# Four small edits in a transformer layer: where head sums are stored from, when ACT's tables are loaded, how the last projection fetches its heads, and how the last store leaves

## The chip, the cores and the metric

The kernel runs on one core of a Trainium2 chip. The metric is the device time of one execution in microseconds. Matrix products run on TensorE (PE), elementwise work on VectorE (DVE), ScalarE (ACT) and GpSimd (POOL), and almost all DMA requests are issued by SyncE (SP), whose queue works in order: a request that waits for its data holds up those behind it. Each engine takes its instructions in the order in which the program wrote them.

## The reference

One encoder layer over a sequence of 2048 rows with 1024 features, all in float32.

```python
mod = c_act @ w_ada[l] + b_ada[l]
sh1, sc1, gt1, sh2, sc2, gt2 = [m[:, None, :] for m in jnp.split(mod, 6, axis=-1)]
h = rmsnorm(x, g_norm1[l]) * (1.0 + sc1) + sh1
proj = h @ w_in[l]
q_sb, k_sb, v_sb, q_ca, k_ca, v_ca = jnp.split(proj, split_pts, axis=-1)
o_sb = stick_breaking_attention(hs(q_sb, ...), hs(k_sb, ...), hs(v_sb, ...))   # 8 heads, strictly causal
o_ca = chunked_relpos_attention(q_ca, k_ca, hs(v_ca, ...), rel_bias[l])        # 8 heads, 9 chunks of 64
mixed = jnp.concatenate([o_sb.reshape(B, S, D_SB), o_ca.reshape(B, S, D_CA)], axis=-1)
x = x + gt1 * (mixed @ w_o[l])
h = rmsnorm(x, g_norm2[l]) * (1.0 + sc2) + sh2
x = x + gt2 * (jnp.square(jax.nn.relu(h @ w1[l])) @ w2[l])
```

## The kernel before, in words

Everything is held transposed, features on partitions, and the sequence is cut into four blocks of 512 (`TB`), called groups `g`. A float32 operand is cut into a high and a low part (`split`: ACT writes the high part, another engine subtracts), and a product is three matmuls (`mm3`). There are three stages.

**Input projections**, up to about 415 us. **Attention**, up to 1285 us: a list of units, each a head `h` and a group `g` (stick-breaking `SB` or chunked `CA`), is worked through in steps, four to a unit. In a step PE makes scores and transposes of weights, ACT a sigmoid (`SB`) or an exponential (`CA`), DVE a scan or a reduction, and POOL a difference or a scaling. Dense matmuls (the rest of the projections, and the output projections `outproj` of groups 3, 2 and 1) are spread into the steps by `fill`; their results leave through tiles `st` of the pool `fp`. Work that has to come later stands in lists: `soon` is done in the next step, `later` counts steps, with its `tick` at a step's end. When both heads of a pair are done, `finish` copies them out of PSUM on ACT, `total` adds two tiles `o` and `otmp` on POOL, and `keep` splits the sum into the tile `os` and stores it to DRAM as `scr_m[g, pair]`. In the kernel before, `os` has one buffer. A step is `turned` where the units change from `SB` to `CA` or back; that is three times, and ACT then needs another table.

**After attention** ("last projection" and MLP). The remaining rows of `outproj` of group 1 are worked off by `row()`, each 24 matmuls `po<-fx,ow`. Between them the requests for the next work are issued: `steps[0].fetch` loads the eight head tiles `opm` of group 0 from `scr_m`, 512 KB each, for the last projection (`Mixed`, matmuls `pso<-opm`), and `some(0, 0)` loads four tiles `ty` of 256 KB with rows of the residual for the first block of the MLP's input. `some(0, 1)` then multiplies and splits them into `h` (`right_blocks`: `scale`, `mixed`, `rest`; four blocks `k`, of which the first works on `ty` and the others on `cy`). While PE runs the eight rows of `Mixed`, DVE and ACT make the four blocks and store residual rows in between; the first products of the MLP (`First`) need all four blocks and a weight split `opr`. The MLP is computed with seven products of a 2x2 block scheme (`PRODUCTS`), `First` and `Second`, twice (`mb` 1, 0). In the last step of `Second` four results `tx` are added on DVE, one after the other, and stored to `out`.

The orders here are written out by hand: after attention every engine's instruction is pinned behind the one written before it, SP's requests too. DMA requests use eight completion semaphores in turn.

Of the kernel before, what the change touches and what calls it, by code (L numbers as in the profile page):

```python
# [10 lines left out]
F32R = mybir.dt.float32r  # L11
BF16 = mybir.dt.bfloat16
AF = mybir.ActivationFunctionType
# [5 lines left out]
P = 128  # L19
# [5 lines left out]
KT = D // P  # L25
TB = 512
# [53 lines left out]
def encoder_kernel(ctx, tc, xT, c, g1, g2, w_in, w_rest, gqk, bias, w_o, w1, w2, w_ada, b_ada, out):  # L80
    nc = tc.nc
    act, dve, pool, sp = nc.scalar, nc.vector, nc.gpsimd, nc.sync
# [35 lines left out]
    zero = cpool.tile([P, 1], F32, name="zero")  # L118
# [9 lines left out]
    cols = cpool.tile([P, 184], F32, name="cols")  # L128
# [7 lines left out]
    later = Later()  # L136

    def split(hi, lo, src, lo_eng=None):
        act.copy(hi, src)
        (lo_eng or dve).tensor_tensor(lo, src, hi.bitcast(F32), op=ALU.subtract)  # L140
# [63 lines left out]
    def mm3(ps, st_hi, st_lo, mv_hi, mv_lo, first, last, more=False):  # L204

        pe.matmul(ps, st_hi, mv_hi, start=first, stop=False, skip_group_check=more)
        pe.matmul(ps, st_hi, mv_lo, start=False, stop=False, skip_group_check=more)
        pe.matmul(ps, st_lo, mv_hi, start=False, stop=last, skip_group_check=more)
# [36 lines left out]
    if True:  # L245
# [257 lines left out]
        act, dve, pool = (Ordered(tc, e) for e in (act, dve, pool))  # L503
# [124 lines left out]
        sp = osp  # L628
# [77 lines left out]
    ph = ctx.enter_context(ExitStack())  # L706
    if True:
# [8 lines left out]
            out=held[:, :P], in_=held[:, :P], pattern=[[1, P]], base=0, channel_multiplier=-1,  # L716
# [4 lines left out]
        sp = nc.sync  # L721
# [33 lines left out]
        def total(u, o, tmp):  # L755

            pool.tensor_tensor(o, o, tmp, op=ALU.add)
            soon.append(lambda: soon.append(lambda: keep(u, o)))

        def keep(u, o):  # L760

            os = op.tile([P, 2, TB], F32R, tag="os", name=f"os{u.nm}", bufs=1)
            split(os[:, 0, :], os[:, 1, :], o, pool)
            q = act if u is units[-1] else sp
            q.dma_start(scr_m[u.g, u.ca * 4 + u.h // 2], os.bitcast(F32))
            pairs[u.g] += 1
            if pairs[u.g] == KT and u.g > 0:
                filler.append(Filler(outproj, u.g))
# [48 lines left out]
        class SB(Unit):  # L817
# [13 lines left out]
            def load(self):  # L831
                if self.first:
                    pend["q"] = load_q(0, self.h, self.g)
                    pend["last"] = [None] * 4
                self.q = pend["q"]
                self.carry = pend["last"]
                if pend.get("k0") != (self.h, self.c):
                    pend["k"] = kp0.tile([P, TB], F32R, tag="k0", name=f"k0{self.nm}")
                    load_k(0, self.h, self.c, 1, pend["k"])
                    pend["k0"] = self.h, self.c  # L840
                self.k = pend["k"]
# [338 lines left out]
        late, soon, first, second = [], [], [], []  # L1180
# [26 lines left out]
        def force(f):  # L1207

            got = next(f.gen, None)
            if callable(got):  # L1210
                got()
            return None if got is None else callable(got)
# [18 lines left out]
        def value(u, j):  # L1231
            u.values(j)
# [14 lines left out]
        op = ph.enter_context(tc.tile_pool(name="op", bufs=2))  # L1247
        pado = ph.enter_context(tc.tile_pool(name="pado", bufs=1))
        pado.tile([P, 80], F32, tag="pad", name="pado")
        fp = ph.enter_context(tc.tile_pool(name="fp", bufs=3))  # L1250
        wtp = ph.enter_context(tc.tile_pool(name="wtp", bufs=4))
        ldq = sp
        steps = [(u, st) for u in units for st in range(STEPS)]
        for i in range(len(steps) + LAG):
            if i % STEPS == 0:
                if i // STEPS + AHEAD < len(units):
                    load(units[i // STEPS + AHEAD])
            vi = i - VST
            if vi >= 0 and vi % STEPS == 0 and vi // STEPS < len(units):
                units[vi // STEPS].load_values()  # L1260
            front, fs = steps[i] if i < len(steps) else (None, 0)
            back, bs = steps[i - LAG] if i >= LAG else (None, 0)
            done = list(soon)
            soon.clear()
            js = []
            if back is not None:
                nb = len(back.banks)
                js = range(nb * bs // STEPS, nb * (bs + 1) // STEPS)
            for j in js:
                back.transposes(j)  # L1270
            turned = front is not None and i and front.ca != steps[i - 1][0].ca
            if front is not None and not turned:
                front.soft1(fs)
            while first:
                first.pop(0)()
            while second:
                second.pop(0)()
            for j in js:
                back.parts(j)
                late.append((back, j))  # L1280
            if turned:
                front.soft1(fs)
            if front is not None:
                front.soft2(fs)
            for job in done:
                if turned:
                    later.add(3, job)
                else:
                    job()
            while len(late) > AVLAG:  # L1290
                value(*late.pop(0))
            if i + 1 < len(steps):
                u, st = steps[i + 1]
                u.scores(st)
            fill(front.weight if front else 0.6, 6 if turned else 0)
            later.tick()
# [7 lines left out]
    sp = osp  # L1304
# [8 lines left out]
    HK = KT // 2  # L1313
# [5 lines left out]
    if True:  # L1319
# [21 lines left out]
        def column_sum(eng, out, a, b, op):  # L1341
            eng.tensor_tensor(out, a, b, op=op)
            return out
# [4 lines left out]
        def kept(nm):  # L1348
            return accp.tile([P, TB], F32, tag="c", name=f"c{nm}")

        def bank(nm):
            return pp.tile([P, TB], F32, tag="ps", name=f"ps{nm}")

        steps, jobs = [], {}
# [92 lines left out]
        class Step:  # L1447
# [5 lines left out]
            def run(self):  # L1453
                pass
# [120 lines left out]
        class Second(Step):  # L1575
# [27 lines left out]
            def run(self):  # L1603
                mb, i, j = self.mb, self.i, self.j
                if j == 0:
                    Second.banks[i] = [bank(f"{self.nm}_{n}") for n in range(HK)]
                if i not in (1, 6, 5):
                    if j == NP // 2 - 1:
                        self.load_base()
                    if NP // 2 + 2 < j <= NP // 2 + 2 + HK:  # L1610
                        self.base(j - NP // 2 - 3)
                for n in range(HK):
                    ns = slice(n * P, (n + 1) * P)
                    mm3(
                        Second.banks[i][n], self.w[:, 0, ns], self.w[:, 1, ns], self.h[:, 0, :], self.h[:, 1, :],
                        j == 0, j == NP - 1,
                    )
                if j == NP - 1:
                    for n in range(HK):
                        self.out(n, Second.banks[i][n])  # L1620

            def load_base(self):
                i, d = self.i, Second.whole
# [8 lines left out]
                x, u = d["x", n], d[{7: "v", 2: "s", 3: "v", 4: "u"}[i], n]  # L1632
                dve.scalar_tensor_tensor(x, u, mod[:, 5 * KT + nn : 5 * KT + nn + 1], x, op0=ALU.mult, op1=ALU.add)

            def out(self, n, ps):
                i, d = self.i, Second.whole
                tb = 2 * self.mb + (i in (2, 4))
                if i == 1:
                    d["s", n] = kept(f"s{self.nm}_{n}")
                    act.copy(d["s", n], ps)  # L1640
                    return
                if i == 6:
                    d["u", n] = column_sum(dve, kept(f"u{self.nm}_{n}"), ps, d["s", n], ALU.add)
                    return
                if i == 5:
                    d["v", n] = column_sum(dve, kept(f"v{self.nm}_{n}"), ps, d["u", n], ALU.add)
                    return
                if i == 7:
                    column_sum(dve, d["u", n], ps, d["u", n], ALU.add)
                nn = n + HK * (i in (7, 4))  # L1650
                x = d["x", n]
                dve.scalar_tensor_tensor(x, ps, mod[:, 5 * KT + nn : 5 * KT + nn + 1], x, op0=ALU.mult, op1=ALU.add)
                sp.dma_start(out[nn * P : (nn + 1) * P, tb * TB : (tb + 1) * TB], x)

        class Mixed(Step):

# [44 lines left out]
        for mb in (1, 0):  # L1701
            begin = len(steps)
            steps += [First(mb, j, i) for j in range(NP) for i in PRODUCTS]
            for j in range(NP):
                f = steps[begin + 7 * j]
# [22 lines left out]
        def some(k, *ns):  # L1728
            for n in ns:
                blocks[k][n]()  # L1730
# [3 lines left out]
        def row():  # L1734

            while force(left) is False:
                pass
            while len(stores) > 2:
                stores.pop(0)()
            return force(left)  # L1740

        row()
        steps[0].fetch(0, KT // 2)
        row()
        some(0, 0)
        steps[0].fetch(KT // 2, KT - 2)
        row()
        some(0, 1)
        steps[0].fetch(KT - 2, KT)
        row()  # L1750
        some(0, 2)
        some(1, 0)
# [75 lines left out]
```

## Time and profile before

| | us |
|---|---|
| median of three runs (2583.73, 2585.42, 7018.68) | 2585.42 |
| the profiled execution's own time | 2585.82 |
| its span, first to last instruction | 2583.9 |
| PE busy | 2568.3 |
| DVE / ACT / POOL busy | 1875.9 / 1393.5 / 903.3 |
| mean granted TensorE clock | 0.997 |

The page's helper line (L42) stands for nearly all instructions, since one wrapper issues them; rows are told apart by tile names. In a row of the timeline the first two numbers are start and duration in us, "x4" is a count of merged instructions, and a bracket at the end is the idle time of the engine just before, and what ended it. The profiled execution's own time is 1.9 us longer than its span, and lies 0.4 us over the median.

### The profile page before, as it was taken

How to read it: one execution, taken by the hardware profiler on the slowest of the kernel's cores; microseconds unless marked ns; L12 is line 12 of the kernel's file. 1: busy time of each engine (PE TensorE's matmuls, PEld its weight loads, DVE VectorE, ACT ScalarE, POOL GpSimd, SP SyncE). 2: the span in 40 equal slices, each digit the busy share in tenths (PEclk: the TensorE clock that was granted, in tenths of full speed). 3: DMA queues.
4: the chain of work that ended last, by engine and by line, in shares of the span. 5: the costliest groups of instructions: out<-in, count | busy, mean ns of one | idle time of the engine just before them, and what ended most of it. 6: DMA issues, size and time to landing. Idle time of an engine off the chain costs nothing. (4 is left out here: it accounts for less than half of the span.)

```text
span 2583.9 us, 39233 instructions
## 1 busy us (share of the span) xinstructions
PE 2568.3 (99%) x12857; PEld 2159.6 (84%) x12857; DVE 1875.9 (73%) x3108; ACT 1393.5 (54%) x2591; POOL 903.3 (35%) x1225
## 2 busy tenths in 40 slices
PE   9999999999999999999999999999999999999999
PEld 7888888888889988888878888888888888888887
DVE  7656767887778899898678778768766665655655
ACT  6333434678886666666744444556544444544443
POOL 4330144666666667666503333100003323100000
PEclk9999999999999999999999999999999999999999
DMA  9879977888887686767697777866764343475574
GB/s 351 317 295 364 342 295 256 256 267 272 270 249 230 208 269 196 250 189 228 210 341 252 262 261 258 317 251 241 248 234 154 143 170 144 148 247 196 196 272 151
DMA packets 253311, 632.86 MB, mean 245 GB/s; under 512 B 28209, under 2 KB 59953, under 8 KB 243250
## 3 DMA queue, kind: packets, MB, share of 16 engines
q1 hardware_dynamic: 251808, 625.62, 70.4%
q10 hardware_dynamic: 1298, 4.72, 0.4%
q8 instruction: 102, 1.67, 0.3%
q14 instruction: 103, 0.84, 0.1%
HBM read 438.87 MB, written 191.37 MB: 244 GB/s over the span
## 5 line engine op out<-in xcount | busy, mean ns | idle before, releaser
L42 PE MATMUL ps<-oph,opv 128*128 128x512 f32 x2688 | 612.4, 389 | 0.5 <-ACT opv L42 0.3
L42 PE MATMUL ps<-h,opw 128*128 128x512 f32 x2664 | 604.2, 389 | 0.0
L42 PEld LDWEIGHTS ps<-oph,opv 128*128 128x128 f32 x2688 | 503.8, 188 | 107.2 <-DVE opv L42 1.2
L42 PEld LDWEIGHTS ps<-h,opw 128*128 128x128 f32 x2664 | 500.0, 188 | 103.8
L42 POOL TENSOR_TENSOR b<-p 128x512 f32<-128x512 f32 (+1 forms) x320 | 292.5, 914 | 200.7 <-DVE p L42 118.0
L42 ACT CAST wth<-wt 128x512 fp32r<-128x512 f32 (+1 forms) x432 | 244.0, 567 | 173.2 <-PE wt L42 168.5
L42 DVE TENSOR_TENSOR wtl<-wt,wth 128x512 fp32r<-128x512 f32 (+1 forms) x432 | 279.8, 651 | 65.5 <-ACT wth L42 64.6
L42 DVE TENSOR_TENSOR oph<-hw,oph 128x512 fp32r<-128x512 f32 x224 | 155.3, 693 | 212.3 <-ACT oph L42 212.3
L42 PE MATMUL pt<-w,ht 128*128 128x512 f32 x1248 | 288.2, 391 | 0.0
L42 ACT CAST oph<-hw 128x512 fp32r<-128x512 f32 x224 | 139.3, 622 | 274.1 <-PE ps L42 269.4
L42 POOL TENSOR_TENSOR ts<-w 128x512 f32<-128x512 f32 x32 | 45.4, 1418 | 667.0 <-DMA w<-in_w_dram 587.9
L42 PEld LDWEIGHTS pt<-w,ht 128*128 128x128 f32 x1248 | 232.9, 188 | 47.7
L42 DVE TENSOR_TENSOR_SCAN p<-z,p,zero 128x512 f32<-128x512 f32 x192 | 245.6, 1280 | 31.2 <-ACT z L42 21.8
L42 PE MATMUL acc<-wth,v 128*128 128x512 f32 (+3 forms) x544 | 217.3, 404 | 0.0
L42 ACT ACTIVATE z<-z 128x512 f32<-128x512 f32 (+1 forms) x320 | 165.8, 520 | 62.6 <-PE z L42 58.7
L42 PE MATMUL z<-k,q 128*128 128x512 f32 (+3 forms) x640 | 183.6, 369 | 2.3 <-DVE p L42 2.0
L42 DVE TENSOR_TENSOR opw<-w,opw 128x512 fp32r<-128x512 f32 x127 | 103.3, 815 | 113.2 <-ACT opw L42 113.1
L42 PE MATMUL acc<-wtl,v 128*128 128x512 f32 (+3 forms) x544 | 181.1, 347 | 0.0
L42 POOL TENSOR_TENSOR e<-e,cols 128x640 f32<-128x640 f32 (+1 forms) x128 | 143.1, 1122 | 92.5 <-DVE cols L42 73.7
L42 PE MATMUL wt<-ident,b 128*128 128x128 f32 x1088 | 165.9, 272 | 0.9 <-DVE wtl L42 0.7
L42 PE MATMUL po<-fx,ow 128*128 128x512 f32 x576 | 162.0, 393 | 0.0
L42 DVE TENSOR_TENSOR opv<-hw,opv 128x512 fp32r<-128x512 f32 x224 | 155.6, 695 | 0.6 <-ACT opv L42 0.6
(195 smaller groups left out, 4072.6 us busy)
## 6 DMA issues: line engine op xcount, KB each, us to landing
hw<-scr_hid SPq DMA_DIRECT2D x112, 512.0 KB, 3.7
q<-scr_q SPq DMA_DIRECT2D x128, 256.0 KB, 4.6
w<-in_w_dram SPq DMA_DIRECT2D x64, 512.0 KB, 5.2
hw<-scr_s SPq DMA_DIRECT2D x64, 512.0 KB, 4.5
fw<-scr_w SPq DMA_DIRECT2D x28, 1024.0 KB, 6.9
k<-scr_k SPq DMA_DIRECT2D x224, 128.0 KB, 4.3
v<-scr_v SPq DMA_DIRECT2D x112, 256.0 KB, 4.3
wa<-in_w_ada_dram SPq DMA_DIRECT2D x48, 512.0 KB, 7.9
```

The costliest lines, as they stand in the source:

```text
L42: return lambda *x, **y: self.tc.keep_in_program_order(f(*x, **y))
```

## The change

- `keep` takes its tile from the pool `fp` with the tag `st`, which is that of the dense stores, and `fp` gets a fourth buffer; `os` and its own buffer are gone. `keep` is put on `later` with four ticks, where it stood on `soon` twice.
- In a turned step, a one-column activation (exponential or sigmoid) is issued on ACT ahead of the step's `soft1`.
- The second half of the eight head tiles of the last projection is fetched at once, ahead of `some(0, 0)`; before, two were fetched behind `some(0, 0)` and two behind `some(0, 1)`.
- The very last output tile is added and stored in two halves of 256 columns, the first stored from ACT's queue and the second from SP's.

```diff
         def total(u, o, tmp):
             pool.tensor_tensor(o, o, tmp, op=ALU.add)
-            soon.append(lambda: soon.append(lambda: keep(u, o)))
+            later.add(4, lambda: keep(u, o))
         def keep(u, o):
-            os = op.tile([P, 2, TB], F32R, tag="os", name=f"os{u.nm}", bufs=1)
+            os = fp.tile([P, 2, TB], F32R, tag="st", name=f"os{u.nm}")
             split(os[:, 0, :], os[:, 1, :], o, pool)
...
-        fp = ph.enter_context(tc.tile_pool(name="fp", bufs=3))
+        fp = ph.enter_context(tc.tile_pool(name="fp", bufs=4))
...
             if turned:
+                act.activation(cols[:, 1:2], zero, AF.Exp if front.ca else AF.Sigmoid)
                 front.soft1(fs)
...
                 if j == NP - 1:
                     for n in range(HK):
-                        self.out(n, Second.banks[i][n])
+                        if self is steps[-1] and n == HK - 1:
+                            for m, q in enumerate((act, sp)):
+                                self.out(n, Second.banks[i][n], slice(m * TB // 2, (m + 1) * TB // 2), q)
+                        else:
+                            self.out(n, Second.banks[i][n])
...
-            def out(self, n, ps):
+            def out(self, n, ps, t=slice(0, TB), q=None):
...
-                x = d["x", n]
+                x, ps = d["x", n][:, t], ps[:, t]
                 dve.scalar_tensor_tensor(x, ps, mod[...], x, op0=ALU.mult, op1=ALU.add)
-                sp.dma_start(out[nn * P : (nn + 1) * P, tb * TB : (tb + 1) * TB], x)
+                (q or sp).dma_start(out[nn * P : (nn + 1) * P, tb * TB + t.start : tb * TB + t.stop], x)
...
         row()
         steps[0].fetch(0, KT // 2)
         row()
+        steps[0].fetch(KT // 2, KT)
         some(0, 0)
-        steps[0].fetch(KT // 2, KT - 2)
         row()
         some(0, 1)
-        steps[0].fetch(KT - 2, KT)
         row()
         some(0, 2)
```

## The prediction

> **What bounds the kernel now.** I read the page first, then PE's waits, then the timelines around the places that the diff touches.
>
> ```profile
> span 2583.9 us, 39233 instructions
> PE 2568.3 (99%) x12857; PEld 2159.6 (84%) x12857; DVE 1875.9 (73%) x3108; ACT 1393.5 (54%) x2591; POOL 903.3 (35%) x1225
> PE z L42 <- DVE p L42: 2.0, 6, 0.6
> PE pso L42 <- DMA opm<-scr_m: 1.6, 2, 1.4
> PE cz L42 <- DVE wtl L42: 1.4, 2, 0.9
> ```
>
> PE is busy for 2568.3 of 2583.9 us, so no edit that leaves the matmuls as they are can win more than 15.6 us (0.6%), but for what a lowered clock costs inside the busy time. The three waits listed are the stalls that the first three edits aim at, 5.0 us together. A measurement of this kernel tells about 2%, 52 us, from no change. The question is which of these few microseconds come back, and what becomes late instead.
>
> **Head sums in the dense stores' tiles.** `os` has one buffer, so ACT's cast waits until the store before has landed.
>
> ```profile
> 476.71 0.62 ACT L42 CAST os<-o 128x512 fp32r<-128x512 f32 x1 [1.51 <-DMA scr_m<-os]
> 481.52 0.73 PE L42 MATMUL z<-k,q 128*128 128x512 f32 x2 [0.64 <-DVE p L42]
> 697.19 0.62 ACT L42 CAST os<-o 128x512 fp32r<-128x512 f32 x1 [1.85 <-DMA scr_m<-os]
> 700.40 0.72 PE L42 MATMUL cz<-k,q 128*128 128x512 f32 x2 [0.94 <-DVE wtl L42]
> ACT os L42 <- POOL o L42: 5.9, 10, 1.4
> ```
>
> This happens twice; PE stands 0.64 and 0.94 us two to four us later. With four tiles shared by both kinds of store those waits go: 1.6 us. ACT also waits ten times, 5.9 us in all, for POOL's sum; four ticks later that sum is done. ACT is far from full, so I take 0.5 us of PE time for it, between -0.5 (the 0.62 us cast now lands in front of another step's work) and 1.5 (a quarter of 5.9). Nothing is added: the same cast, subtraction and store run one to two steps later. Sum: **-2.1 us**.
>
> **Tables in waits.**
>
> ```profile
> 573.26 1.28 ACT L42 ACT_TABLE_LOAD   x1 [1.80 <-DVE cols L42]
> 576.73 0.73 PE L42 MATMUL cz<-k,q 128*128 128x512 f32 x2 [0.47 <-DVE wtl L42]
> 773.85 1.28 ACT L42 ACT_TABLE_LOAD   x1
> 1198.76 1.28 ACT L42 ACT_TABLE_LOAD   x1 [1.80 <-DVE cols L42]
> ```
>
> At the first and third turn ACT idles 1.80 us for DVE and then loads the table for 1.28 us; put into that idle time the load costs nothing, and the exponential starts 1.28 us earlier. At the first turn PE waits 0.47 us behind that chain: gained. At the third no PE wait follows, at the second there is no idle time in front of the load. The one-column activations are tiny and stand beside idle ACT time. **-0.5 us** (0 to -1.2, the 0.47 with the larger half of the cz waits).
>
> **Heads in one request.** This is where I expect the sign to be set.
>
> ```profile
> 1283.35 0.32 SPq L42 DMA_DIRECT2D ow<-scr_wo  x1
> 1284.43 2.34 SPq L42 DMA_DIRECT2D opm<-scr_m  x4
> 1290.42 0.32 SPq L42 DMA_DIRECT2D ow<-scr_wo  x1
> 1297.15 0.33 SPq L42 DMA_DIRECT2D txr<-in_xT_dram  x1
> 1297.52 3.29 SPq L42 DMA_DIRECT2D ty<-scr_x  x4
> 1300.85 0.91 SPq L42 DMA_DIRECT2D opm<-scr_m  x2
> 1303.03 2.03 SPq L42 DMA_DIRECT2D opm<-scr_m  x2
> 1312.15 0.97 PE L42 MATMUL pso<-opm,ow 128*128 128x512 f32 x3 [1.36 <-DMA opm<-scr_m]
> 1310.00:1313.40 3.40, 1.77 (x8) 0.82 (x6) 3.40 (x7) 1.43 (x3) 0.00 (x0) 1.00 1.03 404
> 1313.40:1316.80 3.40, 3.40 (x8) 2.72 (x9) 3.32 (x6) 1.45 (x3) 0.00 (x0) 0.51 1.05 402
> 1316.80:1320.00 3.20, 3.20 (x15) 2.59 (x15) 2.16 (x5) 3.20 (x6) 0.00 (x0) 0.99 1.05 333
> ```
>
> The stretches give time, then busy us (count) of PE, PEld, DVE, ACT, POOL, then granted clock, DMA share and GB/s. The last four heads are requested at 1300.85 and 1303.03, behind the four `ty`; the seventh is late, PE stands 1.36 and 0.28 us (the waits' 1.6), and then the clock is 0.51 for one stretch. In 6.8 us 16 matmuls start where, at 3.2 us for 15, about 32 would: the stall costs 3.4 us in all. Asked for at 1297.5 with the others, the heads land in time and this goes.
>
> But what does PE reach 3.4 us earlier? The `First` steps, whose inputs DVE makes out of `ty` and `cy`:
>
> ```profile
> 1301.91 1.36 DVE L42 TENSOR_TENSOR ty<-ty,r 128x512 f32<-128x512 f32 x2 [5.23 <-DMA ty<-scr_x]
> 1306.14 0.69 DVE L42 TENSOR_TENSOR ty<-ty,r 128x512 f32<-128x512 f32 x1 [1.35 <-DMA ty<-scr_x]
> 1351.43 1.52 DVE L42 TENSOR_TENSOR opr<-w,opr 128x512 fp32r<-128x512 f32 x1
> 1353.90 5.60 PE L42 MATMUL ps<-h,opr 128*128 128x512 f32 x24
> 1308.00:1354.00 46.00, 44.37 (x188) 35.94 (x187) 41.25 (x65) 25.16 (x41) 2.83 (x2) 0.96 0.97 347
> ```
>
> DVE waits 5.23 us for the first `ty` and 1.35 us for the last, which comes at 1306.14; from there it is busy 41.25 of 46 us (its rests are mostly ACT's casts between its own operations) and writes the split that `First` needs at 1352.95. PE begins `First` at 1353.90. So DVE's chain is only 0.95 us ahead of PE: **no more than 0.95 of the 3.4 us can be won**, and a last `ty` that is later by d moves `First` by d - 0.95. The edit puts four heads, 2 MiB (2.1 MB), ahead of `ty` in SP's order, and DMA has nothing to spare there:
>
> ```profile
> 1284.00:1296.00 12.00, 12.00 (x58) 10.08 (x57) 1.00 (x3) 1.78 (x3) 2.58 (x2) 1.00 1.01 352
> 1296.00:1308.00 12.00, 12.00 (x55) 9.94 (x54) 4.08 (x6) 3.48 (x5) 0.00 (x0) 1.00 0.93 316
> ```
>
> 2.1 MB take 6.0 us at 352 GB/s (5.2 at the 404 of the stretch above, 6.6 at 316); the 7% that are free in the second stretch give back at most 0.8. So d is 5.2 from this alone, 4.4 to 6.6.
>
> **What the first edit does here.** The sum of the second-to-last pair of heads is added by POOL at 1278.20, in the step that is fourth from the end of the attention loop. Two steps later, in that step's jobs, ACT casts it; with four ticks `keep` runs at the end of the last step, behind that step's two copies:
>
> ```profile
> 1278.20 1.28 POOL L42 TENSOR_TENSOR o<-o,otmp 128x512 f32<-128x512 f32 x1 [4.81 <-ACT o L42]
> 1280.78 0.62 ACT L42 CAST os<-o 128x512 fp32r<-128x512 f32 x1
> 1281.48 1.30 POOL L42 TENSOR_TENSOR os<-o,os 128x512 fp32r<-128x512 f32 x1 [2.00 <-ACT os L42]
> 1283.42 0.58 ACT L42 COPY o<-acc 64x512 f32<-64x512 f32 x1
> 1282.81 0.32 SPq L765 DMA_DIRECT2D scr_m<-os  x1
> ```
>
> The cast goes from 1280.78 to 1284.00, the store from 1282.81 to 1286.0, and since SP works in order the weights `ow` at 1283.35, four heads and all that follows wait behind it: 3.2 us later, in a DMA stretch with a share of 1.01. It adds to d, which is then 8.4, and the last `ty` comes at 1314.5. Without it d is 5.2. PE may also wait for the `ow` of 1290.42, up to 3.2 us, but that is spent before `First`, where it has to wait for DVE anyway.
>
> So `First` starts 8.4 - 0.95 = 7.4 us later: **+7.4**. PE, standing there for several us, should then see what it saw after its 1.6 us: one stretch of 3.4 us at half clock, **+1.7** (0 to 3.4). The Trainium skill, page "TensorE: Matmul & The Clock Gate", section "Why this matters for your kernels", asks for no idle gaps over about 3 us to keep the clock; by it the 1.6 us of before should have cost no clock. The trace differs (0.51 granted), and the sum goes by the trace; for the longer stall both say a drop.
>
> **Last store in halves.**
>
> ```profile
> 2577.10 2.79 DVE L42 SCALAR_TENSOR_TENSOR tx<-ps,mod,tx 128x512 f32<-128x512 f32 x4 [4.91 <-PE ps L42]
> 2577.88 2.37 SPq L42 DMA_DIRECT2D out_dram<-tx  x4
> 2579.00:2581.00 2.00, 0.10 (x1) 0.00 (x0) 0.89 (x2) 0.00 (x0) 0.00 (x0) 1.00 1.04 362
> ```
>
> Half of the last tile can leave half an addition earlier, 0.35 us (2.79 / 4 / 2). But DMA is full just then (1.04) with the three stores before it, and the second half still waits for the whole addition and one request. I take **-0.2**, from -0.6 to +0.5 (one more addition's start-up and two requests of half-length rows). The Trainium skill, page "DMA: Bandwidth & Descriptors", section "Issuing engines are not separate DMA queues", says that requests from two engines run on the same 16 DMA engines and save only issue time; by it the second queue brings no more than one issue, 0.3 us.
>
> **The sum.** -2.1 - 0.5 + 7.4 + 1.7 - 0.2 = +6.3 on the profiled execution's 2585.82, thus 2592.1; that execution is 0.4 over the median of 2585.42, so **2591.7 us** is what I predict.
>
> **The rivals.**
>
> *The rows are not late enough to matter.* If the last `ty` lands before about 1307.1 (0.95 us after now), all gains stand: -2.1 - 0.5 - 0.95 - 0.2 = -3.75, 2581.7 us. For it: PE's own stall is plain in the trace and the edit removes it; requests from one queue overlap on 16 engines. Against it: 2.1 MB at the highest rate seen here take 5.2 us. This is the not-slower side; the point is the landing of the last `ty`.
>
> *Only the heads delay the rows, the store does not*, because SP's requests in attention are not pinned and something else sets their start. Then d is 5.2: -2.1 - 0.5 + 4.25 - 0.2 = +1.45 and 0 to 1.7 for the clock: 2587 to 2588.6.
>
> *The shared tiles make ACT wait.* Dense casts now wait for head stores. Two such waits cost PE 0.64 and 0.94 us; ten of them over attention would be 8 us on top of the forecast, 2600 us. It decides where stores land later than four uses of a tile apart. Against it: the casts at 476.71 and 697.19 waited for the store just before, not for one four uses back.
>
> *The table load does not move*, if no load is placed before the one-column activation: +0.5 us, inside every range.
>
> **How the numbers follow.** Forecast 0.55, its own range 2588 to 2597 (d from 6.5 to 10, clock 0 to 3.4, and the other terms to their upper ends); only the heads 0.15; rows in time 0.2; shared tiles 0.07; the rest 0.03. The range over the cases is 2580.5 to 2597. All lie within 2% of 2585.42 (2533.7 to 2637.1): same 0.97, slower 0.02, faster 0.01.
>
> **What would show it.** Right: no ACT wait on `scr_m<-os`, no PE wait on `opm`; the store of the second-to-last pair directly ahead of the first `ow` of the tail; DVE's wait for `ty` ending at about 1314 less the 2.6 us gained before; PE waiting several us for `opr` before its first `ps<-h,opr`, with a lowered clock behind it. Wrong: `First` beginning earlier than now, which would mean that DVE's chain had room, or that DMA took the heads faster than any row here shows.

## The result and the profile after

| | before | after |
|---|---|---|
| median of seven runs, us | 2583.73 | 2592.31 |
| ratio after to before, 95% interval | | 1.0038 (1.0026 to 1.0049) |
| span of the profiled execution, us | 2583.9 | 2589.9 |

The change costs 0.38%, 9.8 us (6.7 to 12.7), well inside the 2% that count as no change. One of the seven times of before is 7018.68; the ratio does not use it.

The page and PE's waits of the kernel after (us in total, times, longest):

```profile
span 2589.9 us, 39266 instructions
PE 2567.5 (99%) x12857; PEld 2159.6 (83%) x12857; DVE 1874.4 (72%) x3109; ACT 1395.4 (54%) x2594; POOL 901.1 (35%) x1225
```

```profile
PE ps L42 <- issue: 5.6, 1, 5.6
PE z L42 <- DVE p L42: 2.9, 9, 0.6
PE po L42 <- DMA ow<-scr_wo: 2.2, 1, 2.2
```

The waits for `opm` and for the `cz` scores are gone from the list; those of `z` for `p` grew from 2.0 to 2.9 us. In their place stand 5.6 us before the first product of the MLP and 2.2 us for weights `ow`. SP's queue shows where both begin:

```profile
1284.20 0.32 SPq L765 DMA_DIRECT2D scr_m<-os  x1
1284.61 0.39 SPq L42 DMA_DIRECT2D ow<-scr_wo  x1
1285.82 2.28 SPq L42 DMA_DIRECT2D opm<-scr_m  x4
1288.71 0.32 SPq L42 DMA_DIRECT2D ow<-scr_wo  x1
1295.89 0.33 SPq L42 DMA_DIRECT2D txr<-in_xT_dram  x1
1296.27 2.73 SPq L42 DMA_DIRECT2D opm<-scr_m  x4
1299.04 3.52 SPq L42 DMA_DIRECT2D ty<-scr_x  x4
```

The head sum's store stands directly ahead of the first `ow`, and the four heads ahead of the four `ty`. What follows on DVE, POOL and PE, in order of time:

```profile
1301.73 7.34 PE L42 MATMUL po<-fx,ow 128*128 128x512 f32 x24 [2.18 <-DMA ow<-scr_wo]
1307.78 2.67 DVE L42 TENSOR_TENSOR ty<-ty,r 128x512 f32<-128x512 f32 x4 [12.82 <-DMA ty<-scr_x]
1348.24 0.69 DVE L42 TENSOR_TENSOR cy<-cy,cy 128x512 f32<-128x512 f32 x1
1348.39 1.68 POOL L42 TENSOR_TENSOR ts<-w 128x512 f32<-128x512 f32 x1 [60.57 <-DVE h L42]
1348.84 1.78 DVE L42 TENSOR_TENSOR h<-cy,h 128x512 fp32r<-128x512 f32 x1
1353.42 1.71 POOL L42 TENSOR_TENSOR ts<-w,ts 128x512 f32<-128x512 f32 x1
1353.93 1.74 DVE L42 TENSOR_TENSOR cy<-cy,cy 128x512 f32<-128x512 f32 x1
1356.80 1.45 DVE L42 TENSOR_TENSOR h<-cy,h 128x512 fp32r<-128x512 f32 x2
1357.44 0.61 ACT L42 CAST opr<-w 128x512 fp32r<-128x512 f32 x1
1358.15 1.19 PE L42 MATMUL ps<-h,opr 128*128 128x512 f32 x2 [5.56 <-issue]
1359.57 6.74 PE L42 MATMUL ps<-h,opr 128*128 128x512 f32 x19 [0.23 <-DVE opr L42]
```

DVE waits for all four `ty` until 1307.78, and the last multiplication begins at 1309.76 (the first at 1307.78; the four take 2.67), where it began at 1306.14 before. From there the chain of multiplications and splits runs to the last `h`, which ends at 1358.25. PE begins `First` at 1358.15, just before that end. What the "issue" wait ends with is ACT's cast `opr<-w`, done at 1358.05: it stands in ACT's order behind the last casts `h<-cy`, and these wait for DVE's chain. In e1, below, the profile names this cast. `First`'s third matmul then waits 0.23 us for DVE's part of `opr`. Near its end the chain meets POOL's sums `ts` for the MLP's first weights, and operations that take DVE 0.69 us alone take 1.74 to 1.78 beside them. The clock (time and length of the stretch; busy us and count of PE, PEld, DVE, ACT, POOL; granted clock; DMA share; GB/s):

```profile
1297.00:1309.00 12.00, 9.82 (x37) 7.62 (x36) 1.22 (x2) 0.49 (x1) 0.00 (x0) 0.86 1.03 414
1357.30:1364.10 6.80, 5.72 (x13) 4.11 (x14) 6.41 (x11) 4.13 (x9) 0.00 (x0) 0.50 0.61 189
```

The second stretch is the clock of 0.50 at the 5.56 us, which begins 0.9 us before that wait ends; the 0.86 in the first is 3.4 us at 0.5, at 1302.7, behind the 2.18 us.

The other edits, on ACT at the first turn and at the end of attention, then the end of the program:

```profile
570.43 1.28 ACT L42 ACT_TABLE_LOAD   x1
572.23 0.83 ACT L42 ACTIVATE e<-s,cols 128x640 f32<-128x640 f32 x1 [0.30 <-DVE cols L42]
1282.18 0.62 ACT L42 CAST os<-o 128x512 fp32r<-128x512 f32 x1
...
2583.02 2.92 DVE L42 SCALAR_TENSOR_TENSOR tx<-ps,mod,tx 128x512 f32<-128x512 f32 x5 [4.90 <-PE ps L42]
2585.57 0.34 ACTq L42 DMA_DIRECT2D out_dram<-tx  x1
```

The load now stands ahead of the wait for `cols`. ACT's cast of the head sum follows the step's copies and waits for nothing; no `os` cast waits for `scr_m<-os` any more.

### The profile page after: what moved, and what is told of

It reads as the page before. It is cut to its first block, busy times and chain, and to the rows that moved or that the text cites. A ratio compares the mean times of both kernels' runs of the same rounds, so it can differ in the third digit from the quotient of the medians.

```text
span 2589.9 us, 39266 instructions
## 1 busy us (share of the span) xinstructions
PE 2567.5 (99%) x12857; PEld 2159.6 (83%) x12857; DVE 1874.4 (72%) x3109; ACT 1395.4 (54%) x2594; POOL 901.1 (35%) x1225
## 4 chain that ended last, share of the span: by engine, by line
PE 93%; DVE 2%; DMA 2%; ACT 1%; issue 1%; POOL 1%; SPq 0%; DVEq 0%; POOLq 0%; ACTq 0%
PE ps L42 46%; PE pt L42 11%; PE acc L42 7%; PE wt L42 7%; PE pf L42 5%; PE po L42 5%; PE z L42 4%; PE pq L42 3%; PE cz L42 2%; PE pso L42 1%; DVE p L42 1%; PE ct L42 1%; PE px L42 1%; DMA ow<-scr_wo 0%; POOL b L42 0%
## 5 line engine op out<-in xcount | busy, mean ns | idle before, releaser
L42 PEld LDWEIGHTS wt<-ident,b 128*128 128x128 f32 x1088 | 132.7, 140 | 28.0 <-DVE wtl L42 2.6
```

Of the source, the lines that this page charges most:

```text
L42: return lambda *x, **y: self.tc.keep_in_program_order(f(*x, **y))
```

## The experiments

All times in the tail are counted from the end of attention, taken as the start of its last matmul `acc<-wtl,v` (1284.61 in the profile of before, 1282.89 after). "Last ty" is the start of the last multiplication of `ty`, "opr" the end of DVE's first `opr<-w,opr`, "third First" the start of the first matmul `ps<-h,opw`, behind the two waits of `First` and their clock. "Chain" is opr less last ty. The ratio is to runs of before on the same chip.

| kernel | last ty | opr | chain | third First | wait before First | half clock there | ratio (95%) |
|---|---|---|---|---|---|---|---|
| before, as profiled | 21.5 | 68.3 | 46.8 | 74.7 | none | none (3.4 at `opm`) | |
| e11: before again | 20.4 | 67.7 | 47.3 | 72.9 | 0.70 | none | 0.9996 (0.9987 to 1.0005) |
| e8: tables only | 19.9 | 67.2 | 47.3 | 72.4 | 0.69 | none | one run |
| after | 26.9 | 76.6 | 49.8 | 83.9 | 5.56 | 6.8 (and 3.4 at `ow`) | 1.0038 (1.0026 to 1.0049) |
| e1: heads only | 26.5 | 76.4 | 49.9 | 83.0 | 6.71 | 6.8 | 1.0033 (1.0023 to 1.0044) |
| e2: all but heads | 22.3 | 69.8 | 47.5 | 75.0 | 0.91 | none | 1.0003 (0.9994 to 1.0012) |
| e3: rows first | 22.2 | 70.6 | 48.4 | 75.8 | 1.82 | none | 1.0009 (0.9999 to 1.0018) |
| e4: early store | 26.1 | 75.8 | 49.8 | 82.2 | 7.16 | 6.8 | 1.0031 (1.0020 to 1.0041) |
| e5: rows first, early store | 20.3 | 71.1 | 50.8 | 78.2 | 4.11 | 6.8 | 1.0015 (1.0006 to 1.0025) |
| e6: rows before all heads | 13.8 | 73.5 | 59.7 | 79.6 | 4.77 | 3.4 | 1.0015 (1.0006 to 1.0025) |
| e7: POOL's sums later | 27.2 | 74.6 | 47.4 | 81.3 | 1.92 + 2.04 | 3.4 (and 3.4 at `ow`) | 1.0032 (1.0019 to 1.0044) |
| e9: e5 and e7 | 21.1 | 69.8 | 48.7 | 77.8 | 1.13 + 2.04 | 6.8 | 1.0009 (1.0000 to 1.0018) |
| e10: old order, early store | 19.6 | 67.1 | 47.5 | 72.3 | 1.07 | none | 1.0003 (0.9994 to 1.0013) |

**e1, the third edit alone on the kernel before:**

```diff
+        steps[0].fetch(KT // 2, KT)
         some(0, 0)
-        steps[0].fetch(KT // 2, KT - 2)
         row()
         some(0, 1)
-        steps[0].fetch(KT - 2, KT)
```

> The kernel before with the third edit alone (all four later heads requested ahead of the four rows). Late rows (my theory): the last row tile lands 4 to 6 us later, First starts 4 to 6 us later with several us of PE waiting and a stretch at half clock: +4 to +7 us against before, nothing gained in attention. If the loss of the changed kernel came from the shared store tiles or the table loads in attention: this kernel is at or under before, 0 to -3 us, since PE's wait for the heads is gone.

SP's request for the rows and DVE's work on them:

```profile
1300.06 3.54 SPq L42 DMA_DIRECT2D ty<-scr_x  x4
1309.05 2.57 DVE L42 TENSOR_TENSOR ty<-ty,r 128x512 f32<-128x512 f32 x4 [12.59 <-DMA ty<-scr_x]
...
PE ps L42 <- ACT opr L42: 6.7, 1, 6.7
```

This edit alone makes the kernel slower by 0.33%, 0.23 to 0.44: as much as the whole change within the intervals, and at 8.5 us (5.9 to 11.4) rather more than the 4 to 7 expected. Last ty is at 26.5 without any late store. The last line is PE's wait before `First`: it ends with ACT's cast `opr`.

**e2, the change without its third edit**, on the kernel after:

```diff
-        steps[0].fetch(KT // 2, KT)
         some(0, 0)
+        steps[0].fetch(KT // 2, KT - 2)
         row()
         some(0, 1)
+        steps[0].fetch(KT - 2, KT)
```

> The changed kernel without the third edit (two heads behind the rows, two behind the next step, as before). Late rows: most of the loss goes; what is left is the store of the second-to-last pair, which comes 1.5 to 3 us later and delays the rows by as much, against 1.7 us gained in attention: -1 to +2 us against before. Loss in attention: still +5 to +8 us.

```profile
PE po L42 <- DMA ow<-scr_wo: 2.6, 1, 2.6
...
1303.36 2.60 DVE L42 TENSOR_TENSOR ty<-ty,r 128x512 f32<-128x512 f32 x4 [8.31 <-DMA ty<-scr_x]
1352.84 5.32 PE L42 MATMUL ps<-h,opr 128*128 128x512 f32 x22 [0.91 <-DVE opr L42]
```

The loss is gone: 1.0003. The late store still makes PE wait 2.60 us for `ow`, but `First` starts without a long wait.

**e3, the order of two requests,** on the kernel after:

```diff
-        steps[0].fetch(KT // 2, KT)
         some(0, 0)
+        steps[0].fetch(KT // 2, KT)
```

> The changed kernel with one pair of lines exchanged: the four rows are requested ahead of the four heads, which stay in one request. Late rows: DVE's wait for the rows ends about 4 us earlier than in the changed kernel and First starts 4 to 7 us earlier: -1 to +2 us against before, and the heads are still in time, since they are asked for earlier than the last two were before. Heads in one request as such (their burst on the DMA engines): like the changed kernel, +6 to +9 us.

It comes to 1.0009, so moving four requests past four others takes back most of the loss, and e2 and e3 cannot be told apart.

**e4, the late store taken away:** as after, with the last pairs stored as early as before.

```diff
-            later.add(4, lambda: keep(u, o))
+            if u.ca and u.g == 0:
+                soon.append(lambda: soon.append(lambda: keep(u, o)))
+            else:
+                later.add(4, lambda: keep(u, o))
```

> The changed kernel with the sums of the last eight heads' pairs (group 0, chunked) kept two steps after their addition, as before; all other sums stay at four ticks and in the shared tiles. If the late store of the second-to-last pair adds its delay to the rows, as the prediction had it: the store is issued 1.4 to 3 us earlier, the wait of PE for the projection's last weights shrinks from 2.2 us to under 0.7, and First starts 1.4 to 3 us earlier: 1.4 to 4 us under the changed kernel. If the store's delay is taken up elsewhere: no difference from the changed kernel.

```profile
1279.76 0.32 SPq L768 DMA_DIRECT2D scr_m<-os  x1
1280.30 0.32 SPq L42 DMA_DIRECT2D ow<-scr_wo  x1
1294.26 0.33 SPq L42 DMA_DIRECT2D txr<-in_xT_dram  x1
1305.67 2.64 DVE L42 TENSOR_TENSOR ty<-ty,r 128x512 f32<-128x512 f32 x4 [12.04 <-DMA ty<-scr_x]
1356.01 1.19 PE L42 MATMUL ps<-h,opr 128*128 128x512 f32 x2 [7.16 <-issue]
```

Counted from the end of attention, `ow` is requested 3.0 us earlier than after (-1.3 where it was 1.7), but the next `txr` only 0.3 earlier (12.7, was 13.0). In both, SP stands there for the landing of another store, that of the last pair. ACT issues that store 4.97 us after the end of attention in either kernel, it lands after 12.7 and 13.0 us, and `txr` is requested right then. SP's waits of e4, of after and of before, one each:

```profile
SPq L42 <- DMA scr_m<-os: 6.5, 1, 6.5
```

```profile
SPq L42 <- DMA scr_m<-os: 6.8, 1, 6.8
```

```profile
SPq L42 <- DMA scr_m<-os: 6.4, 1, 6.4
```

So nine tenths of the store's 3.0 us are absorbed in that wait before `ty` is asked for. The wait of 6.4 us was in the profile of before, ahead of the `txr` at 1297.15, and could have been read there. Last ty moves by 0.8, and the ratio of 1.0031 can't be told from that of after: rival "only the heads delay the rows" holds for the store's part.

**e5, both causes undone:** e4 with e3's order.

> All four edits, but the four rows ahead of the four later heads, and the last pairs' sums kept after two steps: both causes of late rows undone. Late rows: PE's wait of 2.2 to 2.6 us for the projection's last weights goes, the heads come in time, and First starts where DVE's chain lets it, about 0 to 1 us earlier than in the kernel before when measured from the end of attention; with 1.7 us from attention the span is 2580 to 2582.5, 1.5 to 4 us under before. If the rows were not the cause: as the changed kernel, 2587 to 2592.

```profile
1342.72 1.39 POOL L42 TENSOR_TENSOR ts<-w 128x512 f32<-128x512 f32 x1 [55.92 <-DMA w<-in_w_dram]
1342.88 1.78 DVE L42 TENSOR_TENSOR cy<-cy,cy 128x512 f32<-128x512 f32 x1
1351.60 1.19 PE L42 MATMUL ps<-h,opr 128*128 128x512 f32 x2 [4.11 <-issue]
```

With last ty as early as in before (20.3) it still lost 0.15% (0.06 to 0.25), where a gain of 1.5 to 4 us was expected. POOL's first sum meets the chain, and it is DVE that is held: the chain is 50.8 long instead of 47.4, PE waits 4.11 us, and the clock halves for 6.8. Of the 3.4 us more, 1.0 is a wait of DVE for the residual rows `txr`, which now come behind four heads; the rest is the meeting with POOL.

Who is held can be told by counting from DVE's first `h` of the last block. Where POOL's first sum begins 1.2 to 2.3 us after it (after, e1, e4, e5, e6), DVE is held and needs 12.5 us from that `h` to the end of `opr`. Where it begins 4.1 to 4.4 us after it (e3, e8, e10, e11), POOL is held (its row stands under e8) and DVE needs 10.1 to 10.2. Where it begins 6.1 us or more after it (e2, e7, e9, before), DVE needs no more than that. Where between 2.3 and 4.1 us this turns, and why, no run shows.

**e6, the rows ahead of all eight heads:** e4 with this order of requests.

```diff
         row()
-        steps[0].fetch(0, KT // 2)
-        row()
-        steps[0].fetch(KT // 2, KT)
         some(0, 0)
+        steps[0].fetch(0, 2)
+        row()
+        steps[0].fetch(2, KT)
         row()
```

> As the kernel with rows first and early keep, but the rows go ahead of all eight heads (rows, two heads, then after the next row of the projection six heads). If DVE's chain from the rows is what bounds First, it now starts 5 us or more earlier, PE never waits for it, and what the stall on the heads cost (3.4 us) becomes a gain: span 2576.5 to 2580, 4 to 7 us under before. If First is bound by something else (weights of the MLP, POOL's sums): no better than with rows first, 2580 to 2582.5. If the heads are now late: a PE wait on them, and a lowered clock.

```profile
1293.77 2.49 DVE L42 TENSOR_TENSOR ty<-ty,r 128x512 f32<-128x512 f32 x4
1310.77 0.75 DVE L42 SCALAR_TENSOR_TENSOR txr<-po,mod,txr 128x512 f32<-128x512 f32 x1 [5.10 <-DMA txr<-in_xT_dram]
1315.22 2.50 DVE L42 TENSOR_TENSOR cy<-cy,r 128x512 f32<-128x512 f32 x4
```

`ty` is there 12 us sooner, but DVE, whose order is fixed, then waits twice for the residual rows `txr` (5.67 and 5.10 us), and the next block's `cy` is multiplied only at 1315.22. POOL's sums hold DVE here too. The bound moved from `ty` to what is loaded behind the heads; 4 to 7 us of gain were expected, and the ratio is 1.0015 (1.0006 to 1.0025), no better than e5's.

**e7, POOL's sums one step later:** as after, with `fetch`, which loads and sums the MLP's first weights, put off by one.

```diff
-                steps[n + LEFT].load() if n + LEFT < KT else steps[KT].fetch() if n + LEFT == KT else None
+                steps[n + LEFT].load() if n + LEFT < KT else steps[KT].fetch() if n + LEFT == KT + 1 else None
```

> The changed kernel with the first weights of the MLP loaded, and so POOL's four sums of them made, one row of the last projection later (5.5 us). In the changed kernel DVE's operations take 1.74 to 1.78 us in place of 0.69 while POOL makes these sums at 1348 to 1355. If POOL's work slows DVE: those DVE operations take 0.69 us again, First starts 2 to 3.6 us earlier, though its second product may then wait for POOL's sums: -1 to -3 us against the changed kernel. If DVE's slow operations have another cause (DMA writes, PE at rest): they stay slow at the same place, and nothing is won.

```profile
1351.10 0.69 DVE L42 TENSOR_TENSOR cy<-cy,cy 128x512 f32<-128x512 f32 x1
1354.66 1.09 DVE L42 TENSOR_TENSOR opr<-w,opr 128x512 fp32r<-128x512 f32 x1
1355.80 6.82 PE L42 MATMUL ps<-h,opr 128*128 128x512 f32 x22 [2.04 <-DVE opr L42]
```

With the sums out of the way DVE's rows are back at 0.69, but for the last `h` and `opr` (1.60 and 1.09), and the chain is 47.4: 2.4 us of the lateness came from the collision. In time it can't be told from after: 1.0032 and 1.0038, with intervals of about 0.0012 to either side, and 2.4 us are 0.0009.

**e8, the second edit alone**, one run.

```diff
             if turned:
+                act.activation(cols[:, 1:2], zero, AF.Exp if front.ca else AF.Sigmoid)
```

> The kernel before with the second edit alone, one look. The load of the tables stands in ACT's idle time at the first and third turn; PE's wait of 0.47 us behind the first turn goes; attention ends 0.3 to 0.8 us earlier. If the load still stands behind DVE's result: nothing changes. The time itself is within its noise of before.

One run of 2581.29, beside a median of 2581.43 for before on that chip. Its tail is that of before, but the stall on `opm` isn't there, and POOL's first sum, 1.4 to 1.8 us in after, e4 and e5, takes 3.76 beside a chain that keeps its 0.69 us up to the last `h`:

```profile
1309.73 11.85 PE L42 MATMUL pso<-opm,ow 128*128 128x512 f32 x51 [0.16 <-DMA opm<-scr_m]
1343.86 3.76 POOL L42 TENSOR_TENSOR ts<-w 128x512 f32<-128x512 f32 x1 [56.23 <-DMA w<-in_w_dram]
```

**e9, e5 with e7's line.**

> All four edits, with the rows ahead of the later heads, the last pairs' sums kept after two steps, and POOL's first sums one row later. With rows first and early keep, PE was early (no stall on heads), so the weights came early, and POOL's sums ran beside the end of DVE's chain and slowed it (three operations at 1.75 to 1.78 us): 4.1 us of PE waiting and 6.8 us at half clock. If that is why that kernel did not win: DVE's operations stay at 0.69 us, First starts 2 to 4 us earlier after attention's end than there (69.7 us), with under 2 us of waiting, and the time is 3 to 6 us below that kernel's ratio of 1.0015: 0.9990 to 1.0003. If not: as there, 1.0010 to 1.0020.

Opr comes 1.3 sooner than in e5 and `First` begins 2.6 sooner. But PE's waits are 1.13 and 2.04 us, more than the 2 expected, and the clock still halves for 6.8 us; 1.0009 (1.0000 to 1.0018) lies between the two outcomes that were named. That is nearer to before than e5, by less than the two intervals allow to tell.

**e10, e4 with the old order of heads:** the first, second and fourth edit, with the early store.

> The changed kernel with the heads fetched in the old order and the last pairs' sums kept after two steps: only the shared tiles, the table loads and the halved store differ from before. Attention and store as such: between the first transpose and the last product of attention 0.3 to 0.8 us less than before (860.5 us); at the end nothing; tail as before. -2 to +1 us, ratio 0.9992 to 1.0004. If the shared tiles or the halved store cost time by themselves: over 1.0008.

1.0003 (0.9994 to 1.0013), with a tail like that of before: last ty 19.6, third First 72.3. The three edits without the heads bring nothing that shows.

**e11, before again**, to see how far two runs of one kernel differ.

> The kernel before, unchanged, timed against itself and profiled again. Its ratio should hold 1; the interval shows what these comparisons can tell. The profile shows how much of the kernel before varies from run to run: whether the clock at the start (10.2 us at half rate in its first profile, 3.4 us in the changed kernel's) and the stall on the heads (1.36 us) are there again.

```profile
478.02 0.62 ACT L42 CAST os<-o 128x512 fp32r<-128x512 f32 x1 [4.61 <-DMA scr_m<-os]
1313.17 11.86 PE L42 MATMUL pso<-opm,ow 128*128 128x512 f32 x51 [0.23 <-DMA opm<-scr_m]
1353.38 5.30 PE L42 MATMUL ps<-h,opr 128*128 128x512 f32 x22 [0.70 <-DVE opr L42]
```

Two runs of one kernel give 0.9996, an interval of 0.09% to either side. The stall on `opm` is 0.23 us here, with full clock, where the first profile had 1.36 and 0.28 us and a halved stretch. ACT's wait for the store is 4.61 us here, where it was twice 1.5 to 1.9. No version was faster than before; the intervals of e2, e3 and e10 hold 1.

## Why the prediction was right, and where not

2592.31 was measured for 2591.7 forecast. What sets the sign is what the runs show, the heads ahead of the rows. That the number fits so closely is luck in part, since errors of two to three us cancel in it. The difference is less well met: +6.3 was forecast on the profiled execution and +6.0 is what the two profiles give, but over many runs it is 9.8 (6.7 to 12.7). The forecast's start was 1.7 us too high, since the median of three stood at 2585.42 and that of seven at 2583.73.

*The heads ahead of the rows.* Right, mechanism and size. Last ty is later by 4.6 us with the late store in both (after less e2) and by 6.4 without it (e4 less e10), for 5.2 forecast. e1 shows that this edit is enough, and e3 that the order of the requests is what counts, not the joining of four heads into one request.

*The late store, 3.2 us more.* This term was mis-sized. It happened as described, 3.0 us at the `ow` request, but SP then waits for the last pair's store in either case (e4). Last ty moved by 0.8 us (after less e4), 2.7 with the old order (e2 less e10), 1.9 with the rows first (e3 less e5). The sign named for it did not come: DVE's wait for `ty` was to end at about 1311.4, and it ended at 1307.78. The two causes do not add: d was 6.8 from the mean of e8 and e11, 5.3 from the first profile, not 8.4. So the rival "only the heads", with 5.2 and a chance of 0.15, came nearer to the delay of the rows than the forecast.

*PE's base.* The stall on `opm` that the edit should remove, 3.4 us with its clock, is the forecast's weakest reading. It was a chance of that execution: in e8 and e11 it is 0.16 and 0.23 us, with no clock lost. PE had next to nothing to win there, so the comparison with the usual execution comes out worse than that with the profiled one.

*DVE's chain.* That a late chain moves `First` was right. The 0.95 us of room was not: it was counted to `First`'s first matmul, but it is the third that waits for DVE's `opr`, and that began at 1354.36 in the profile of before, 1.41 us behind the chain. In e8 and e11, where PE isn't held by `opm`, there is no room at all: PE waits 0.69 and 0.70 us for `opr`. That a late chain loses to POOL's sums was not foreseen: they begin 38.5 to 38.6 us after last ty in after, e1 and e4, where the chain is 49.8 to 49.9 long, and 41.3 or more in e2, e7, e8, e10 and e11, where it is 47.3 to 47.5 (in e3, e5 and e9 it also holds 0.9 to 1.3 us of waiting for `txr`). e7, which moves the sums alone, shows it. The Trainium skill, page "SBUF — State Buffer", section "Who interferes with whom", says that a DVE instruction with two inputs in SBUF contends with a GpSimd instruction that reads SBUF, and that the order of issue decides which of the two blocks. The trace of after agrees: POOL's sum of 1348.39 ends at 1350.07, and DVE's `h`, begun at 1348.84, ends 0.55 us after that. In e8 the starts alone do not tell it: `cy<-cy,cy` begins at 1343.97, 0.11 us behind POOL's sum, and still takes 0.69 us.

*The clock.* One stretch was forecast, 1.7 us; there were three, 3.4 us behind the wait on `ow` and 6.8 at the one before `First`. PE is busy for 3.4 and 5.72 us of them, so they cost some 4.6 us of full speed. Of the first, little reaches the end, since PE waits before `First` anyway. Against the mean of e8 and e11 the third step of `First` is 11.3 us later: 6.8 for last ty, 2.4 for the chain and 2.1 for the clock and the rest of `First`. That agrees with the 9.8 measured, less what attention gives.

*Attention, -2.6.* The waits of ACT on `scr_m<-os` are gone in all nine kernels with shared tiles, as forecast, and ACT's ten waits for POOL's sum are one in after. From the first `wt<-ident,b` to its end attention takes 859.8 to 860.4 us in these nine; in the four kernels without it 860.5 (before), 860.8 (e8), 863.2 (e1) and 863.3 (e11), on average 1.8 more. In the last two ACT's cast waits 4.4 and 4.6 us for the store, DVE's `p` waits for ACT, and PE some 3 us for `p`; then comes a stretch at half clock. Here of e11:

```profile
PE wt L42 <- DVE p L42: 3.1, 1, 3.1
```

```profile
481.30:484.70 3.40, 3.40 (x11) 2.35 (x10) 3.40 (x5) 1.17 (x2) 2.21 (x4) 0.51 0.95 318
```

So the size is about right, the reason is another than I priced: it is the long wait that two of the four show, not the short ones. Between the two profiles attention gains only 0.2 us; the waits of `z` for `p` are 2.9 us in all nine kernels, more than the 2.0 of before. The tables' part, at most 0.5, could not be told from this.

*The halves, -0.2.* From the start of PE's last matmul to the end of the span it is 5.17 to 5.22 us without them (four kernels) and 5.25 to 5.29 with them (nine). They cost some 0.07 us.

*The two profiles, added up.* From before to after: the end of attention 1.7 earlier (1.5 of it since attention began that much sooner, where no edit had come yet), third First 9.2 later from there, the rest of the MLP 1.6 shorter, the last store 0.1 longer: +6.0. For `First` with its clock 9.1 was forecast (8.4 - 0.95 + 1.7). The 9.2 are made of other parts: 5.3 for last ty, 3.0 for the chain and 0.9 for the rest. A store taken for too much and a collision that stood in no sum cancel, and that is luck, as are the 1.5 us ahead of attention. Of the 1.6, 0.6 are waits for `opv` and `ndgm` that PE no longer has; where the other 1.0 is from stays open. Of the rivals, "rows in time" fell with e1, "shared tiles make ACT wait" with the page of after, "the table load does not move" with the row at 570.43.

What also stays open is whether some order of these requests beats before. e5, e6 and e9 each took a cause away and met the next: POOL's sums (e5), the later `txr` and `cy` (e6), the clock (e9).

## What to carry to other kernels

A wait that is seen once in one execution is not yet a gain: profile the unchanged kernel a second time before pricing its removal. When requests are joined, ask what they now stand ahead of in the queue, and whether the engine that waits for those has room; here it had little over one microsecond in one execution and none in two others, and the queue's order moved the rows by 4.6 to 6.4. And a chain that is made late also meets new neighbours: look at what the other engines do in the time into which it is moved.

## What the runs showed of the hardware that was not expected

- The clock dropped behind short waits, and not behind all: 1.36 and 0.28 us (before), 2.18 us (after), 2.50 us (e7) and 3.1 us (e11) were followed by 3.4 us at half clock, but 2.60 us in e2 and 2.51 in e3 by none. With waits of 4.1 to 7.2 us came 6.8 us at half clock, of which 0.9 to 2.9 still lay in the wait; with that of 4.77 in e6 only 3.4, from its end on. The rule of the Trainium skill that the prediction weighed, page "TensorE: Matmul & The Clock Gate", section "Why this matters for your kernels", has about 3 us as the bound; in these runs no single bound fits.
- A stretch at half clock that begins 7.7 to 10.2 us after the start of the program, ahead of every edit, was 3.4, 6.8 or 10.2 us long, and in e7 it was missing; two runs of one kernel had 10.2 and 6.8.
- The wait for one and the same store of a head sum was 1.5 us in one execution and 4.6 in another of the same kernel (before, e11).
